# A paced weight cast before the memory keys, a later split of mem, and a last row tile that is normalized in PSUM

## The chip, the cores and the metric

The kernel runs on one core of a Trainium2 chip. The core has engines that each run their own instructions in order: TensorE (matmuls, PE in the profile, with its weight loads as PEld), VectorE (DVE), ScalarE (ACT), GpSimd (POOL), and SyncE (SP), which here issues the DMAs. They wait for each other through semaphores. SBUF is the working memory; PSUM holds what TensorE writes, in banks of 512 fp32 columns. The metric is the device time of one execution in microseconds (us), the median of several runs.

## The reference, cut to what matters

One decoder layer on 256 tokens of width 1024, all in fp32: one input projection feeds a causal pooling mixer and an attention of 8 heads; then come an output projection with LayerNorm, a cross-attention into 256 memory tokens with LayerNorm, and a SwiGLU block with LayerNorm.

```python
z = h @ w_in[l]                                  # u, q, k, v: 512 columns each
pool_out = multiscale_pool(u, w_pool[l], pool_scale[l])
attn_out = moba_attention(q, k, v).reshape(B_, S_, ATTN_WIDTH)
mix = jnp.concatenate([pool_out, attn_out], axis=-1) @ w_out[l]
h = layer_norm(DEEPNORM_ALPHA * h + mix, ln1_g[l], ln1_b[l])
h = layer_norm(DEEPNORM_ALPHA * h + memory_cross_attention(h, mem, w_xq[l], w_xkv[l], w_xo[l]),
               ln2_g[l], ln2_b[l])
h = layer_norm(DEEPNORM_ALPHA * h + swiglu(h, w_gate[l], w_up[l], w_down[l]), ln3_g[l], ln3_b[l])
```

With 256 tokens there is one attention block, so the attention is plain causal attention. The LayerNorm takes the mean and variance of a row of 1024, then `(x - mu) * rsqrt(var + eps) * g + b`.

## The kernel before, in words

**Numbers in two halves.** Every product of weights is made of three matmuls on fp32r halves: a tensor is split into `hi`, its rounded copy, and `lo`, what the copy lost, and hi*hi, hi*lo and lo*hi are added (`three`, line 232; `proj_t`, line 244). The split costs one copy on ScalarE and one subtraction on VectorE (`split`, line 297, and for weights lines 91 and 92).

**The weight stream.** `Stream` (line 42) holds all weights as 125 numbered tiles of [128, 1024] (the first few are half as wide) in the order of use: w0 to w10 for q and k, w11 to w14 for v, w15 to w18 for u, w19 to w26 for the memory keys (`xk`), w27 to w34 for the output projection, and so on. `fetch` issues a load, `prepare` casts a tile into its halves (w12h, w12l in the profile) and then issues the load seven tiles further. There are eight pairs of hi and lo buffers, so a cast waits until the tile eight before it has been used up. `get` is called once for every group of matmuls on a tile: it makes sure that the tile it needs is cast, and, unless the stream is held, asks for one more, up to eight (`AHEAD`) beyond the tiles that are used up. `held` is set in the projections with LayerNorm and in the last part of q and k. `before` hangs further loads onto a tile's load: the load of x for the residual on w27's.

**Order.** Each engine's order is the program's order (`manual_schedule`). The phase that the change touches is written out by hand in lines 500 to 536. `run(gen, n)` advances one of the generators `v`, `u` and `xk` by n steps of matmuls, and between them stand attention's parts:

- a step of `v` is one `get` and three matmuls of 512 columns, for one row tile and one k; there are 16 of them. A step of `u` or `xk` is three matmuls of 256 columns, and every second step calls `get`: 16 calls for u, 32 for the memory keys.
- `scores(hq, t)` (line 402): eight small matmuls into two banks, then on VectorE a masked maximum (line 416), on ScalarE the exponentials (line 385), on VectorE the scaling (lines 390 to 392).
- `probs_t(hp)` (line 426): six transposes into two banks, then a copy of the first bank on VectorE (line 436) and of the second on ScalarE (line 437).
- `attend(hp)` (line 442): four pairs of small matmuls into a bank, then a split.
- `split_mem(k)` (line 188): the split of half of mem's transpose, [128, 1024], a ScalarE copy and a VectorE subtraction; the memory keys read its halves mTh and mTl, the first half in k = 0 to 3, the second in k = 4 to 7.
- `do_v` ends with two copies of v to SBUF on ScalarE (`vt`, line 482); `do_u` copies each of its chunks to `upad` on ScalarE (line 488), from which GpSimd forms the window sums (`windows`, line 455). `pool_diff(g)` (line 465) takes them on VectorE, and `mix_pool(g)` (line 469) multiplies the result on TensorE.

All these parts take banks from one pool of four (`bank`), the projections take theirs from another four (`accbank`).

**The end.** The last projection (`project`, line 589) first adds the first 16 of its 22 weight tiles into four accumulators, one per row tile of 128 tokens and half of the columns; then it finishes piece after piece over the last six tiles. The last row tile's second half is finished as two pieces of 256 columns, and the last of these goes into a bank of its own, so that its sum is that bank plus what the accumulator holds. `Norm` (line 543) adds each piece to the residual on VectorE (line 557), takes statistics (`bn_stats`, line 560), aggregates them (line 565), and forms the reciprocal root on GpSimd (line 568) while VectorE runs the first two `centre`s (line 572); `scale` (line 577) then writes the output row, which is stored in three parts from SyncE's and ScalarE's queues (line 773).

Of the kernel before, what the change touches and what calls it, by code (L numbers as in the profile page):

```python
# [11 lines left out]
OP = mybir.AluOpType  # L12
# [3 lines left out]
D = 1024  # L16
S = 256
T = S // P
# [9 lines left out]
ALPHA = 2.0 ** 0.25  # L28
# [13 lines left out]
class Stream:  # L42


    def __init__(self, nc, pool):
        self.nc, self.pool = nc, pool
        self.src, self.raws, self.tiles, self.homes = [], [], [], []
        self.loads, self.splits = {}, {}
        self.used, self.held = 0, True

    def add(self, src, parts=2):

        n = src.shape[1] // parts
        first = len(self.src)
        self.src += [src[:, i * n:(i + 1) * n, :] for i in range(parts)]
        return range(first, len(self.src))
# [39 lines left out]
    def get(self, numbers, k):  # L96

        n = self.src[numbers[0]].shape[1]
        self.prepare(numbers[k // n] + 1)
        if not self.held:  # L100
            self.prepare(min(self.used + AHEAD, len(self.tiles) + 1))
        hi, lo = self.tiles[numbers[k // n]]
        return hi[:, k % n, :], lo[:, k % n, :]
# [13 lines left out]
def decoder_layer(  # L117
# [3 lines left out]
    nc = tc.nc  # L121
# [13 lines left out]
    def bank(name):  # L135
        return pb.tile([P, 512], F32, tag="b", name=name)

    def accbank(name):
        return pa.tile([P, 512], F32, tag="acc", name=name)


    ws = Stream(nc, wp)
# [45 lines left out]
    def split_mem(k):  # L188
        split(mT[0][:, k:k + 4, :], mT[1][:, k:k + 4, :], mr[0][:, k:k + 4, :])
# [8 lines left out]
    gb = {}  # L198
# [45 lines left out]
    def proj_t(pss, numbers, yT):  # L244


        for k in range(KD):
            hi, lo = ws.get(numbers, k)
            y_hi, y_lo = pair(yT, ALL, k)
            for f in range(2):  # L250
                s = slice(f * P, (f + 1) * P)
                for n, (w, y) in enumerate(((hi, y_hi), (hi, y_lo), (lo, y_hi))):
                    nc.tensor.matmul(pss[f], w[:, s], y, start=k == 0 and f == 0 and n == 0,  # L253
                                     stop=k == KD - 1 and n == 2, skip_group_check=True)
                if f == 1:
                    ws.done(numbers, k)
                yield
# [10 lines left out]
    def proj_rows(acc, chunks, get, pieces, first, last, free, again=False):  # L268

        last_k = sum(ws.rows(numbers) for numbers in chunks) - 1  # L270
        k0 = 0
        for numbers in chunks:
            nk = ws.rows(numbers)
            for t in sorted({piece[0] for piece in pieces}):
                for j in range(nk):
                    k = k0 + j
                    y = pair(get(k), ALL, slice(t * P, (t + 1) * P))
                    hi, lo = ws.get(numbers, j)
                    for piece in pieces:
                        if piece[0] == t:  # L280
                            s = slice(*piece[1:])
                            three(acc[piece], y, (hi[:, s], lo[:, s]), first and k == 0, last and k == last_k,
                                  again)
                    if free and t == pieces[-1][0]:
                        ws.done(numbers, j)
                    yield
            k0 += nk

    def run(gen, n=None):

        while n is None or n > 0:
            if next(gen, gen) is gen:
                return False
            n = None if n is None else n - 1
        return True

    def split(h, l, ps):
        nc.scalar.copy(h, ps)  # L298
        nc.vector.tensor_sub(l, ps, r32(h))  # L299
# [142 lines left out]
    def attend(hp):  # L442
        s0, s1 = pts[hp]
        po = bank("po")
        for j in range(2):
            hs = slice(j * HD, (j + 1) * HD)
            vs = slice((2 * hp + j) * HD, (2 * hp + j + 1) * HD)
            nc.tensor.matmul(po[hs, :S], vt[:, 0, vs], s0[:, j, :], start=True, stop=False)
            nc.tensor.matmul(po[hs, P:S], vt[:, 1, vs], s1[:, j, :], start=False, stop=True)
        split(cT[0][:, 4 + hp, :], cT[1][:, 4 + hp, :], po[:, :S])  # L450
# [14 lines left out]
    def pool_diff(g):  # L465
        pl = upad[:, g, PADW:]
        nc.vector.scalar_tensor_tensor(pl, sums[g][:, PADW:], 1.0 / WINDOWS[g], pl, op0=OP.mult, op1=OP.subtract)
# [9 lines left out]
    def do_v():  # L477
        pieces = [(t, 0, 512) for t in range(T)]
        acc = {piece: accbank("pv") for piece in pieces}
        yield from proj_rows(acc, c_v, lambda k: (xT[0][:, k], xT[1][:, k]), pieces, True, True, True)  # L480
        for piece in pieces:
            nc.scalar.copy(vt[:, piece[0], :], acc[piece])

    def do_u():
        for c in range(2):
            ps = accbank("pu").rearrange("p (f t) -> p f t", f=2)
            yield from proj_t([ps[:, f, :] for f in range(2)], c_u[c], xT)
            nc.scalar.copy(upad[:, 2 * c:2 * c + 2, PADW:], ps)  # L488
            for f in range(2):
                windows(2 * c + f)  # L490
# [3 lines left out]
    def do_xk():  # L494
        for c in range(4):
            ps = accbank("pxk").rearrange("p (f t) -> p f t", f=2)
            yield from proj_t([ps[:, f, :] for f in range(2)], c_xk[c], mT)
            split(xkT[0][:, 2 * c:2 * c + 2, :], xkT[1][:, 2 * c:2 * c + 2, :], ps)

    v, u, xk = do_v(), do_u(), do_xk()  # L500
    run(v, 2)
    scores(0, 0)
    run(v, 2)
    scores(0, 1)
    run(v)
    run(u, 4)
    split_mem(0)
    probs_t(0)
    run(u, 6)
    scores(1, 0)  # L510
    probs_t(1)
    run(u, 6)
    split_mem(4)
    attend(0)
    run(u, 6)
    scores(1, 1)
    attend(1)
    run(u)
    run(xk, 6)
    pool_diff(0)  # L520
# [9 lines left out]
    attend(2)  # L530
    mix_pool(2)
    pool_diff(3)
    run(xk, 8)
    attend(3)
    mix_pool(3)
    run(xk)


    early.close()
# [3 lines left out]
    class Norm:  # L543
# [23 lines left out]
            nc.vector.tensor_scalar(self.rs, self.mv[:, 1:2], EPS, None, op0=OP.add)  # L567
            nc.gpsimd.tensor_tensor(self.rs, self.rs, mhalf, op=OP.pow)  # L568

        def centre(self, c0, c1):  # L570
            s = slice(c0, c1)
            nc.vector.scalar_tensor_tensor(self.r[:, s], self.r[:, s], self.mv[:, 0:1], gb["g", self.i][:, s],  # L572
                                           op0=OP.subtract, op1=OP.mult)

        def scale(self, c0, c1):
            s = slice(c0, c1)
            nc.vector.scalar_tensor_tensor(self.dst[:, s], self.r[:, s], self.rs, gb["b", self.i][:, s],  # L577
                                           op0=OP.mult, op1=OP.add)

        def finish(self):  # L580
            self.stats()
            for half in HALVES:
                self.centre(*half)
                self.scale(*half)

    HALVES = ((0, 512), (512, D))
# [22 lines left out]
    def until(gen):  # L609

        for got in gen:
            if got is not None:
                return got
# [6 lines left out]
    for t in range(T):  # L620
        norm = Norm(1, xt[:, t, :], h1[:, t, :])
# [78 lines left out]
    h2 = ap.tile([P, T, D], F32, tag="a8", name="h2")  # L700
# [14 lines left out]
    norm = Norm(2, h1[:, 0, :], h2[:, 0, :])  # L715
# [3 lines left out]
    norm = Norm(2, h1[:, 1, :], h2[:, 1, :])  # L719
# [52 lines left out]
    def store(t, y, c0, c1, queue=nc.sync):  # L772
        queue.dma_start(out[t * P:(t + 1) * P, c0:c1], y[:, c0:c1])

    pieces = PIECES[:3] + ((1, 512, 768), (1, 768, D))
    dn = project(c_dn, lambda k: (gT[k // KD][0][:, k % KD], gT[k // KD][1][:, k % KD]), 6, pieces)
    run(dn, 4)
    gated_t(NFC - 1)
    for t in range(T):
        norm = Norm(3, h2[:, t, :])  # L780
        for _, c0, c1 in [piece for piece in pieces if piece[0] == t]:
            acc = until(dn)[1]
            if c1 - c0 == 512:
                norm.add(c0, c0 + 256, acc[:, :256])
                norm.add(c0 + 256, c1, acc[:, 256:])
            elif c0 == 512:
                norm.sum(512, D, acc)
                norm.measure(c0, c1)
            else:
                nc.vector.tensor_add(norm.r[:, c0:c1], norm.r[:, c0:c1], acc)  # L790
                norm.measure(c0, c1)
        norm.stats()
        norm.centre(0, 512)
        norm.centre(512, 768)
        norm.scale(0, 512)
        store(t, norm.r, 0, 512)
        norm.scale(512, 768)
        store(t, norm.r, 512, 768, nc.scalar)
        norm.centre(768, D)
        norm.scale(768, D)  # L800
        store(t, norm.r, 768, D)
    run(dn)


# [36 lines left out]
```

## Time and profile before

| | |
|---|---|
| time, median of 3 runs | 389.57 us (389.51 to 389.97) |
| the profiled execution's own time | 389.37 us |
| its span, from the first to the last instruction | 387.6 us |
| TensorE busy | 376.8 us, 97% of the span |
| VectorE, ScalarE, GpSimd busy | 250.5, 179.6, 17.9 us |
| granted TensorE clock, mean | 0.993 |
| read from HBM | 70.52 MB, 185 GB/s over the span |

The profile is one execution, seen by the hardware profiler. A row of the timeline has the start, the duration, the engine, the line of the program, the operation, output and input by the program's names with their shapes, and in brackets the idle time of the engine ahead of it with what ended it. A duration includes the instruction's latency: the next instruction of the same engine often starts before it is over. Rows of waits have the engine and line that waited, what for, the total in us, how often, and the longest. The view by line has the count, the busy time in us and the mean duration in ns. TensorE's matmuls are pipelined, so their busy time is more than their arithmetic.

### The profile page before, as it was taken

The numbers are of one execution on the slowest core, as the hardware profiler recorded it, in microseconds if no ns is written. First come the engines' busy times: TensorE is split into PE (matmuls) and PEld (weight loads), VectorE is DVE, ScalarE is ACT, GpSimd is POOL, SyncE is SP. The second block draws the span as 40 slices with busy tenths as digits, with TensorE's granted clock in tenths as the row PEclk, the third lists the DMA queues.
The fourth block names the chain that finished last, engine by engine and source line by source line (L and its number), as shares of the span: only waits on it lengthen the run. The fifth ranks groups of instructions, "written<-read, shape, count | busy, mean of one in ns | idle before, by whom it ended". The sixth has DMA issues, their size and how long they took to land.

```text
span 387.6 us, 5472 instructions
## 1 busy us (share of the span) xinstructions
PE 376.8 (97%) x2120; PEld 327.4 (84%) x2120; DVE 250.5 (65%) x361; ACT 179.6 (46%) x262; POOL 17.9 (5%) x31
## 2 busy tenths in 40 slices
PE   8999899999999999999999999999999999999992
PEld 8997779998888899988878888888888888888881
DVE  4768998655589767665889655556465555444176
ACT  5656965543254644545148544545554454343000
POOL 1000036100020000000100000000000000000000
PEclk9999999999999999999999999999999999999997
DMA  7998785438507973443108956565557655630011
GB/s 218 400 406 324 221 323 164 145 113 286 200 1 224 402 230 122 128 145 108 56 0 285 364 169 210 167 193 187 183 197 261 225 165 170 212 108 2 0 41 67
DMA packets 21689, 71.91 MB, mean 186 GB/s; under 512 B 2464, under 2 KB 3232, under 8 KB 21536
## 3 DMA queue, kind: packets, MB, share of 16 engines
q1 hardware_dynamic: 21232, 71.05, 53.8%
q10 hardware_dynamic: 432, 0.52, 0.4%
q8 instruction: 16, 0.26, 0.3%
q14 instruction: 9, 0.07, 0.1%
HBM read 70.52 MB, written 1.05 MB: 185 GB/s over the span
## 4 chain that ended last, share of the span: by engine, by line
PE 94%; DVE 4%; issue 1%; POOL 0%; POOLq 0%; ACT 0%; DVEq 0%
PE pg L236 10%; PE pg L235 10%; PE pg L237 10%; PE acc L237 8%; PE acc L236 8%; PE acc L235 8%; PE pqk L349 6%; PE pxq L253 6%; PE pxk L253 6%; PE pu L253 3%; PE xv L237 2%; PE xv L235 2%; PE xv L236 2%; PE pgt L744 1%; PE busy L323 1%; PE pv L235 1%
## 5 line engine op out<-in xcount | busy, mean ns | idle before, releaser
L568 POOL TENSOR_TENSOR rs<-rs,mhalf 128x1 f32<-128x1 f32 x6 | 5.7, 955 | 307.5 <-DVE rs L567 307.5
L737 ACT ACTIVATE sg<-pg 128x256 f32<-128x256 f32 x22 | 8.4, 384 | 12.9 <-PE pg L237 12.8
L557 DVE SCALAR_TENSOR_TENSOR r<-h,acc 128x256 f32<-128x256 f32 (+1 forms) x11 | 5.9, 534 | 10.9 <-PE acc L237 10.9
L738 DVE TENSOR_TENSOR sg<-sg,pg 128x256 f32<-128x256 f32 x22 | 9.3, 421 | 4.0 <-ACT sg L737 2.6
L385 ACT ACTIVATE pr<-pr,mx 128x128 f32<-128x128 f32 (+1 forms) x16 | 7.1, 444 | 7.3 <-DVE mx L416 7.3
L560 DVE BATCH_NORM_STATS2 st<-r 128x6 f32<-128x512 f32 (+1 forms) x16 | 9.0, 561 | 0.5
L572 DVE SCALAR_TENSOR_TENSOR r<-r,mv,g 128x512 f32<-128x512 f32 (+1 forms) x14 | 9.2, 668 | 0.0
L298 ACT CAST h2Th<-tp 128x512 fp32r<-128x512 f32 x4 | 2.4, 588 | 13.7 <-PE tp L309 13.7
L298 ACT CAST gTh<-pgt 128x512 fp32r<-128x512 f32 x11 | 6.0, 589 | 5.8 <-PE pgt L744 5.8
L385 ACT ACTIVATE xpr<-xs,mx 128x256 f32<-128x256 f32 x8 | 3.7, 470 | 10.2 <-DVE mx L396 10.2
L299 DVE TENSOR_TENSOR gTl<-pgt,gTh 128x512 fp32r<-128x512 f32 x11 | 7.1, 687 | 2.0 <-ACT gTh L298 1.5
L577 DVE SCALAR_TENSOR_TENSOR h<-r,rs,b 128x512 f32<-128x512 f32 x8 | 6.0, 752 | 1.9 <-POOL rs L568 1.8
L460 POOL TENSOR_TENSOR win<-upad 128x271 f32<-128x271 f32 x4 | 3.8, 956 | 55.6 <-ACT upad L488 55.6
L744 PEld LDWEIGHTS pgt<-ident,sg 128*128 128x128 f32 x44 | 5.2, 140 | 0.8
L390 DVE RECIPROCAL sm<-sm 128x2 f32<-128x2 f32 x12 | 2.0, 166 | 5.9 <-ACT xpr L385 4.5
L744 PE MATMUL pgt<-ident,sg 128*128 128x128 f32 x44 | 5.8, 272 | 0.0
L309 PEld LDWEIGHTS tp<-ident,h 128*128 128x128 f32 x32 | 3.8, 141 | 2.0 <-issue 0.7
L298 ACT CAST h1Th<-tp 128x512 fp32r<-128x512 f32 x4 | 2.3, 587 | 6.7 <-PE tp L309 6.7
L299 DVE TENSOR_TENSOR xkTl<-pxk,xkTh 128x512 fp32r<-128x512 f32 x4 | 2.8, 692 | 4.1 <-ACT xkTh L298 4.1
L309 PE MATMUL tp<-ident,h 128*128 128x128 f32 x32 | 4.8, 274 | 0.4 <-DVE h L577 0.3
L323 PE MATMUL busy<-spark 128*128 128x128 f32 x18 | 4.2, 430 | 1.1 <-DVE spark L321 1.1
L298 ACT CAST xkTh<-pxk 128x512 fp32r<-128x512 f32 x4 | 2.3, 587 | 5.9 <-PE pxk L253 5.9
(1087 smaller groups left out, 1421.0 us busy)
## 6 DMA issues: line engine op xcount, KB each, us to landing
g<-in_ln_g SPq DMA_DIRECT2D x3, 512.0 KB, 6.4
b<-in_ln_b SPq DMA_DIRECT2D x3, 512.0 KB, 7.4
wr<-in_w_in SPq DMA_DIRECT2D x5, 256.0 KB, 5.8
mr<-in_mem_t SPq DMA_DIRECT2D x1, 1024.0 KB, 11.1
xt<-in_x SPq DMA_DIRECT2D x1, 1024.0 KB, 8.0
xr<-in_x_t SPq DMA_DIRECT2D x3, 256.0 KB, 7.4
wr<-in_w_in SPq DMA_DIRECT2D x1, 512.0 KB, 7.8
w7r<-in_w_in SPq DMA_DIRECT2D x1, 512.0 KB, 8.2
```

Source lines behind the costliest of these rows:

```text
L235: nc.tensor.matmul(ps, wa, ya, start=start, stop=False, skip_group_check=part)
L236: nc.tensor.matmul(ps, wa, yb, start=False, stop=False, skip_group_check=part)
L237: nc.tensor.matmul(ps, wb, ya, start=False, stop=stop, skip_group_check=part)
L253: nc.tensor.matmul(pss[f], w[:, s], y, start=k == 0 and f == 0 and n == 0, stop=k == KD - 1 and n == 2, skip_group_check=True)
L298: nc.scalar.copy(h, ps)
L299: nc.vector.tensor_sub(l, ps, r32(h))
L349: nc.tensor.matmul(qk[i][:, f, :], w[:, c * P:(c + 1) * P], y, start=k == 0 and f == 0 and n == 0 and w is hi, stop=k == KD - 1 and w is l ...
L385: nc.scalar.activation(dst[:, j, :], src[:, j, :], AF.Exp, bias=mx[:, j:j + 1], scale=sign, accum_out=sm[:, j:j + 1])
L560: nc.vector.bn_stats(self.st[:, self.n, :], self.r[:, c0:c1])
L572: nc.vector.scalar_tensor_tensor(self.r[:, s], self.r[:, s], self.mv[:, 0:1], gb["g", self.i][:, s], op0=OP.subtract, op1=OP.mult)
L738: nc.vector.tensor_mul(sg, sg, ps[:, CW:])
L744: nc.tensor.transpose(pt[:, f, t * P:(t + 1) * P], sgs[c][:, t, f * P:(f + 1) * P], ident)
```

## The change

Three things change.

- `Stream` gets a `pace`: a call of `get` asks for a further cast only where the number of calls so far is a multiple of it. It is 3 from v to the memory keys, 2 for the last part of the keys, and 1 otherwise.
- In the hand-written order, `scores(0, 1)` comes after four further steps of v in place of two, and the two `split_mem` come after `attend(0)` and `attend(1)`.
- In the last row tile, the sum with the residual, the statistics and the centring stay in the PSUM banks of the accumulators, in place; only `scale` writes SBUF. The sum of the last 512 columns becomes two of 256.

```diff
@@ class Stream
+        self.pace, self.asked = 1, 0
...
         self.prepare(numbers[k // n] + 1)
-        if not self.held:
+        self.asked += 1
+        if not self.held and self.asked % self.pace == 0:
             self.prepare(min(self.used + AHEAD, len(self.tiles) + 1))
@@ the order from v to the memory keys
     v, u, xk = do_v(), do_u(), do_xk()
+    ws.pace = 3
     run(v, 2)
     scores(0, 0)
-    run(v, 2)
+    run(v, 4)
     scores(0, 1)
     run(v)
     run(u, 4)
-    split_mem(0)
     probs_t(0)
     run(u, 6)
     scores(1, 0)
     probs_t(1)
     run(u, 6)
-    split_mem(4)
     attend(0)
+    split_mem(0)
     run(u, 6)
     scores(1, 1)
     attend(1)
+    split_mem(4)
     run(u)
...
     pool_diff(3)
+    ws.pace = 2
     run(xk, 8)
     attend(3)
     mix_pool(3)
     run(xk)
+    ws.pace = 1
@@ class Norm: centre and scale take the place of the residual
-        def centre(self, c0, c1):
+        def centre(self, c0, c1, r=None):
             s = slice(c0, c1)
-            nc.vector.scalar_tensor_tensor(self.r[:, s], self.r[:, s], self.mv[:, 0:1], gb["g", self.i][:, s],
+            r = self.r[:, s] if r is None else r
+            nc.vector.scalar_tensor_tensor(r, r, self.mv[:, 0:1], gb["g", self.i][:, s],
                                            op0=OP.subtract, op1=OP.mult)
...
+            r = self.r[:, s] if r is None else r
+            nc.vector.scalar_tensor_tensor(self.dst[:, s], r, self.rs, gb["b", self.i][:, s],
                                            op0=OP.mult, op1=OP.add)
@@ the last projection (the first row tile's work stays as it was)
+    def in_bank(norm, acc, c0, c1):
+
+        nc.vector.scalar_tensor_tensor(acc, norm.tok[:, c0:c1], ALPHA, acc, op0=OP.mult, op1=OP.add)
+        nc.vector.bn_stats(norm.st[:, norm.n, :], acc)
+        norm.n += 1
+
+    norm = Norm(3, h2[:, 1, :])
+    left = until(dn)[1]
+    for c in (0, 256):
+        in_bank(norm, left[:, c:c + 256], c, c + 256)
+    right = until(dn)[1]
+    norm.sum(768, D, right[:, 256:])
+    in_bank(norm, right[:, :256], 512, 768)
+    last = until(dn)[1]
+    nc.vector.tensor_add(last, norm.r[:, 768:], last)
+    nc.vector.bn_stats(norm.st[:, norm.n, :], last)
+    norm.n += 1
+    finish(norm, 1, (left, right[:, :256], last))
```

`finish` is what stood behind the sums before, in the same order: statistics, two centres, a scale and its store, a scale and its store, then the last centre, scale and store; its last argument says where the residual's three parts lie.

More of the change, by code (lines that the diff above doesn't have):

```diff
@@ L568, in stats, with scale @@
             nc.gpsimd.tensor_tensor(self.rs, self.rs, mhalf, op=OP.pow)
-        def centre(self, c0, c1):
+        def centre(self, c0, c1, r=None):
             s = slice(c0, c1)
-            nc.vector.scalar_tensor_tensor(self.r[:, s], self.r[:, s], self.mv[:, 0:1], gb["g", self.i][:, s],
+            r = self.r[:, s] if r is None else r
+            nc.vector.scalar_tensor_tensor(r, r, self.mv[:, 0:1], gb["g", self.i][:, s],
                                            op0=OP.subtract, op1=OP.mult)
-        def scale(self, c0, c1):
+        def scale(self, c0, c1, r=None):
             s = slice(c0, c1)
-            nc.vector.scalar_tensor_tensor(self.dst[:, s], self.r[:, s], self.rs, gb["b", self.i][:, s],
+            r = self.r[:, s] if r is None else r
+            nc.vector.scalar_tensor_tensor(self.dst[:, s], r, self.rs, gb["b", self.i][:, s],
                                            op0=OP.mult, op1=OP.add)
@@ L778, in decoder_layer, with finish @@
     gated_t(NFC - 1)
[L779 to L791, printed above, removed]
+    def finish(norm, t, at):
         norm.stats()
-        norm.centre(0, 512)
-        norm.centre(512, 768)
-        norm.scale(0, 512)
+        norm.centre(0, 512, at[0])
+        norm.centre(512, 768, at[1])
+        norm.scale(0, 512, at[0])
         store(t, norm.r, 0, 512)
-        norm.scale(512, 768)
+        norm.scale(512, 768, at[1])
         store(t, norm.r, 512, 768, nc.scalar)
-        norm.centre(768, D)
-        norm.scale(768, D)
+        norm.centre(768, D, at[2])
+        norm.scale(768, D, at[2])
         store(t, norm.r, 768, D)
+    norm = Norm(3, h2[:, 0, :])
+    for half in HALVES:
+        acc = until(dn)[1]
+        for c in (0, 256):
+            norm.add(half[0] + c, half[0] + c + 256, acc[:, c:c + 256])
+    finish(norm, 0, (None, None, None))
+    def in_bank(norm, acc, c0, c1):
[4 more added lines that the diff above has]
+    left = until(dn)[1]
+    for c in (0, 256):
+        in_bank(norm, left[:, c:c + 256], c, c + 256)
[7 more added lines that the diff above has]
+    finish(norm, 1, (left, right[:, :256], last))
     run(dn)
```

## The prediction

> **What bounds the kernel now.** I read the summary by engine, the busy time by stretch of the span, TensorE's waits, and then the timeline around each wait. First the stretches; the columns are the stretch, its length, TensorE's busy time, and then weight loads, VectorE, ScalarE, GpSimd, granted clock and DMA.
>
> ```profile
> 46.00:50.00 4.00, 2.24 (x21) 1.68 (x20) 3.88 (x5) 2.31 (x4) 0.00 (x0) 1.00 0.97 340
> 50.00:198.00 148.00, 148.00 (x954) 132.83 (x953) 104.92 (x164) 68.60 (x113) 14.53 (x18) 1.00 0.50 169
> 198.00:200.00 2.00, 1.61 (x9) 0.88 (x7) 1.97 (x4) 0.62 (x2) 0.00 (x0) 1.00 0.00 0
> 200.00:380.00 180.00, 179.95 (x834) 150.10 (x834) 101.90 (x119) 78.10 (x96) 0.92 (x1) 1.00 0.51 170
> 380.00:387.60 7.60, 0.00 (x0) 0.00 (x0) 4.35 (x10) 0.00 (x0) 0.92 (x1) 0.64 0.19 69
> ```
>
> The reader is to see that TensorE sets the time: from 50 to 380 us it is without work for only 0.39 + 0.05 us. What can be won without fewer matmuls lies in two places, 4.00 - 2.24 = 1.76 us in the stretch from 46 to 50, and the 7.60 us behind the last matmul, where VectorE alone works. The change touches both. TensorE's waits name what stands in the first:
>
> ```profile
> PE pt L433 <- DVE sb L436: 1.3, 1, 1.3
> PE pt L431 <- ACT sb L437: 0.4, 1, 0.4
> ```
>
> Both are the transposes of probs_t(1), which need the banks of probs_t(0), and these are free only when the copies of line 436 (VectorE) and line 437 (ScalarE) have run. The timeline shows why the copies are late:
>
> ```profile
> 37.92 0.42 DVE L416 CUSTOM_DVE_ANT_0 pr<-ps,tri 128x256 f32<-128x256 f32 x1
> ...
> 41.43 1.23 DVE L92 TENSOR_TENSOR w18l<-w18r,w18h 128x1024 fp32r<-128x1024 f32 x1
> ...
> 44.15 1.06 ACT L482 COPY vt<-pv 128x512 f32<-128x512 f32 x2
> ...
> 46.29 0.71 PE L409 MATMUL ps<-qkT 64*128 64x128 f32 x8
> 47.33 1.22 DVE L299 TENSOR_TENSOR mTl<-mr,mTh 128x1024 fp32r<-128x1024 f32 x1
> 47.42 0.33 PE L431 MATMUL pt<-ident,pr 128*128 128x128 f32 x1 [0.41 <-ACT sb L437]
> 48.46 0.68 DVE L436 COPY sb<-pt 128x512 f32<-128x512 f32 x1
> ```
>
> VectorE's queue behind scores(0,1) holds w18, w19, w20, w21, w22 and mem's first half, and only then the copy, at 48.46. A 1024-wide subtraction holds VectorE for 48.46 - 47.33 = 1.13 us. TensorE asked for the banks at 47.42 - 0.41 = 47.01.
>
> **The change, part by part.** *Casts.* A cast is one copy on ScalarE and one subtraction on VectorE, and it lets one load be issued. None is added or removed: I count the calls of get in the program's order. 16 come before v, so with a pace of 3 v's 16 calls ask at the 18th, 21st, 24th, 27th and 30th for w14 to w18 (before: w14 to w21), and u's 16 calls for w19 to w24 (before: w22 to w25). The pace of 2 and the limit of eight ahead bring the count to w33 at the end of the memory keys, as before, so what follows finds the same state. No call has to make a tile that it needs at once: the keys start with w19 to w24 ready.
>
> *The wait at 47 us.* Two casts now stand ahead of scores(0,1) in place of four, so its first row moves from 37.92 to 37.92 - 2 x 1.13 = 35.7, and its last work, which ended just ahead of w18 at 41.43, to 39.2. TensorE gives scores(0,1) two steps later, which hides in what was won. Then come w16, w17, w18 (to 42.6) and w19, whose ScalarE half stands behind v's copies to vt. They started at 44.15 and can now start when v ends, near 42.0: vt to 43.1, w19's copy, which has as many elements as the two of vt, to 44.1, its subtraction to 45.2, and the copy of line 436 ends at 45.9. TensorE asks at 47.0. mem's first half isn't in front any more. So the wait goes, 1.76 us, with 1.1 us to spare; VectorE would have to lose a whole further cast before any of it came back.
>
> *Mem's split, and what is late next.* Rows for the place where the moved work meets TensorE again:
>
> ```profile
> 55.08 1.14 PE L409 MATMUL ps<-qkT 64*128 64x256 f32 x8
> 56.25 0.42 DVE L416 CUSTOM_DVE_ANT_0 pr<-ps,tri 128x256 f32<-128x256 f32 x1
> ...
> 59.55 0.42 DVE L299 TENSOR_TENSOR cTl<-po,cTh 128x256 fp32r<-128x256 f32 x1
> ...
> 60.65 0.28 PE L253 MATMUL pxk<-mTh,w19h 128*128 128x256 f32 x1
> ...
> 60.85 0.59 ACT L488 COPY upad<-pu 128x512 f32<-128x512 f32 x1 [0.85 <-PE pu L253]
> 62.41 1.53 DVE L92 TENSOR_TENSOR w26l<-w26r,w26h 128x1024 fp32r<-128x1024 f32 x1 [1.16 <-ACT w26h L91]
> 63.87 0.85 DVE L467 SCALAR_TENSOR_TENSOR upad<-win,upad 128x256 f32<-128x256 f32 x1
> 65.62 0.60 PE L471 MATMUL pm<-upad,wpl 128*128 128x256 f32 x2
> ```
>
> All of TensorE's times move 1.76 forward. The keys start at 60.65 - 1.76 = 58.9. Mem's first half comes behind w20, scores(1,0), a copy, w21 and attend(0)'s subtraction, at most 45.9 + 1.13 + 3.30 + 0.68 + 1.13 + 0.42 + 1.13 = 53.7 (3.30 is scores(1,1), with wider rows, below). The second follows attend(1): scores(1,1) can start on VectorE when its products are there, 55.08 + 1.14 - 1.76 = 54.5, about when w22 behind mem's first half is done; 3.30 us from row 56.25 to row 59.55 later comes attend(1)'s subtraction (57.8), its 0.42 to 58.2, mem's 1.13 to 59.3. The keys need it after eight steps. Twelve steps and six transposes lie between 60.65 and 65.62, so eight take about 3 us: needed at 61.9. Hidden, by 2.6 us. But behind it on VectorE stand w23, w24 and w25 (3 x 1.13, to 62.7) and then pool_diff(0), without which mix_pool(0) on TensorE can't start. Before, VectorE stood idle here, 1.16 us ahead of w26, and mix_pool(0) came 65.62 - 63.87 - 0.85 = 0.90 after the end of pool_diff(0). Now mix_pool(0) is due at 65.62 - 1.76 = 63.86. pool_diff(0) ends at 62.7 + 0.42 = 63.1 if it runs undisturbed, and its own line says what that is worth:
>
> ```profile
> L467 DVE SCALAR_TENSOR_TENSOR upad<-win,upad x4: 415/416/846, 63.9 to 75.4; 128x256 f32<-128x256 f32 x4
> ```
>
> The 846 ns and the 1.53 us of w26 (1.23 at w18) fall on GpSimd's window sums of the second u chunk, which run here again. With both, pool_diff(0) ends at 62.7 + 0.30 + 0.85 = 63.9, a new wait of about 0.05 us plus a hand-over; with w23, w24 and mem's half slowed in the same way too, 3 x 0.30 more, about 1.0 us. Undisturbed it is 0. I take **0.15 us**, near the case that the rows show, and keep 0 to 1.0. Loads are issued later by as much as their casts, and x's load with them, with no reader near: the first LayerNorm's sum is past 100 us.
>
> *The last row tile.* The rows behind the last matmul, and the same shapes elsewhere (mean ns behind the comma):
>
> ```profile
> 380.04 0.42 DVE L790 TENSOR_TENSOR r<-r,acc 128x256 f32<-128x256 f32 x1 [0.44 <-PE acc L237]
> ...
> 381.32 1.14 DVE L572 SCALAR_TENSOR_TENSOR r<-r,mv,g 128x512 f32<-128x512 f32 x2
> 381.55 0.92 POOL L568 TENSOR_TENSOR rs<-rs,mhalf 128x1 f32<-128x1 f32 x1 [6.68 <-DVE rs L567]
> 382.51 1.15 DVE L577 SCALAR_TENSOR_TENSOR r<-r,rs,b 128x512 f32<-128x512 f32 x2
> ...
> 384.08 0.48 DVE L577 SCALAR_TENSOR_TENSOR r<-r,rs,b 128x256 f32<-128x256 f32 x1
> ```
>
> ```profile
> L557 DVE SCALAR_TENSOR_TENSOR r<-h,acc 128x256 f32<-128x256 f32 x6 | 2.5, 412 | 9.6 <-PE acc L237 9.6
> L473 DVE SCALAR_TENSOR_TENSOR cTl<-pm,psc,cTh 128x256 fp32r<-128x256 f32 x4 | 1.9, 482 | 0.8 <-ACT cTh L472 0.8
> ...
> L572 DVE SCALAR_TENSOR_TENSOR r<-r,mv,g 128x256 f32<-128x256 f32 x4 | 1.9, 480 | 0.0
> ```
>
> The chain keeps its instructions: one addition, one bn_stats, three centres, three scales, the stores. Only the side on which the residual lies changes. Reading a bank in place of SBUF costs nothing that shows: 482 ns with a PSUM input and a per-row scalar against 480 ns without PSUM. Writing a bank from VectorE occurs nowhere in the trace. The nearest rows are two forms of one instruction that differ in their operands, 412 and 480 ns, so I bound it by 0.07 us for each instruction in either direction. A loss counts for all eight, +0.56. A gain counts for six, -0.42, since the first two centres end at 381.32 + 1.14 = 382.46 and the reciprocal root on GpSimd at 381.55 + 0.92 = 382.47: faster centres would wait for it. I take **0**, as the reads show. Ahead of the last matmul one 256-wide instruction is added (the sum of 512 becomes two); VectorE's 0.44 us of idle time ahead of row 380.04 hides its 0.42. With 0.07 us on each of the six instructions there that touch a bank this cover is gone and up to another 0.4 shows.
>
> [...]
>
> **Sum**, on the profiled execution's own 389.37 us (span 387.60 and 1.77 around it): 389.37 - 1.76 + 0.15 + 0 = 387.76. The median of the runs, 389.57, is 0.20 above that execution, so I predict **387.95 us**.
>
> **Rivals.** *The wait moves to mix_pool(0)* (0.13): VectorE's queue stays disturbed by GpSimd, 1.0 us or more comes back: 389.57 - 1.76 + 1.0 = 388.8, in the worst case nothing is left. For it: 1.53 and 846 ns. Against it: three of four pool_diffs took 416 ns. *The copy is late anyway* (0.05), so that the change doesn't do what it says: 389.5. It needs over 1.1 us more on VectorE ahead of it. *A bank costs VectorE more* (0.10), at the bound: +0.56 and 0.2 of the lost cover, 388.7, still faster. [...] *Slower* (0.05): a write into a bank holds VectorE as long as the disturbed pool_diff, 846 - 416 = 430 ns more, on eight instructions: +3.4, 391.2. It decides from (1.76 - 0.15) / 8 = 0.20 us each, and against it stands that no undisturbed row differs so much.
>
> **How the numbers follow.** The forecast has 0.67. What a measurement can tell here is 0.2%, 0.78 us. Faster than 388.79: the forecast, the costly bank and half of the first rival, 0.67 + 0.10 + 0.06 = 0.83. Within: 0.07 + 0.05 = 0.12. Slower: 0.05. The range reaches from the gain at the tail without a new wait, 389.57 - 1.76 - 0.42 = 387.4, to the first rival with a little of the second bound, 388.9.
>
> **What would show it.** Right: no wait of a transpose for line 436 or 437, TensorE busy throughout 46 to 50; at mix_pool(0) a wait of 0 to 0.3 us or none; the keys start near 58.9; the span from the last matmul to the end within 0.1 of 7.6 us. Wrong: TensorE idle by over 0.5 us before the mix, named as waiting for pool_diff, mem's low half or a cast; centres or scales of the last tile that differ by over 0.07 us from 480 ns at 256 columns.

## The result, and the profile after

The changed kernel takes 388.75 us (median of 8 runs, 388.44 to 388.84), the kernel before beside it 389.96 (8 runs, 389.51 to 391.35). The ratio, that of the means, is 0.9962, with a 95% interval of 0.9948 to 0.9976: 1.5 us faster, between 0.9 and 2.0; the medians differ by 1.21 us. That the two kernels differ is clear; by how much, the runs tell less well than the traces do, because the kernel before spreads: of its 59 executions beside the experiments, 23 show a granted clock of 0.989 or 0.990 and take 390.7 to 392.2 us, and the other 36 show 0.993 to 0.997 and take 389.1 to 390.4.

TensorE's waits after the change:

```profile
PE busy L325 <- DVE spark L323: 1.1, 1, 1.1
PE pm L473 <- DVE upad L469: 0.9, 1, 0.9
PE tp L311 <- DVE h L584: 0.3, 1, 0.3
PE pqk L351 <- ACT w4h L92: 0.2, 1, 0.2
```

Both waits of the transposes are gone, and one stands there that wasn't in the list before: mix_pool(0), line 473, waits 0.9 us for pool_diff(0), line 469. (The first and the third row were there before; the last is a weight that arrives late at the very start, w4, whose copy on ScalarE waited 0.95 us for its load; TensorE waited 0.2 us for it here, 0.8 in run 6, and run 3 lists no such wait.) By stretches, with the columns as before:

```profile
46.00:50.00 4.00, 4.00 (x37) 3.75 (x37) 3.27 (x16) 2.29 (x11) 0.00 (x0) 1.00 0.94 320
58.90:66.00 7.10, 6.21 (x51) 5.92 (x51) 7.04 (x7) 5.08 (x8) 4.15 (x4) 1.00 0.42 130
66.00:196.00 130.00, 130.00 (x813) 116.49 (x812) 91.75 (x125) 58.45 (x87) 7.61 (x9) 1.00 0.50 171
```

From 46 to 50 TensorE now works throughout, where it had stood idle for 1.76 us. The copy of the first bank runs well ahead of the transposes of probs_t(1):

```profile
45.32 0.68 DVE L438 COPY sb<-pt 128x512 f32<-128x512 f32 x1
...
47.40 0.33 PE L433 MATMUL pt<-ident,pr 128*128 128x128 f32 x1
47.56 0.27 PE L434 MATMUL pt<-ident,pr 128*128 128x128 f32 x1
47.67 0.27 PE L435 MATMUL pt<-ident,pr 128*128 128x128 f32 x1
...
48.03 0.36 PE L255 MATMUL pu<-xTh,w16h 128*128 128x256 f32 x1
```

From 58.9 to 66 it misses 0.89 us, while VectorE is busy for 7.04 of 7.10; from 66 to 196 nothing is missing. The timeline of that place, VectorE's rows first, then GpSimd's and TensorE's:

```profile
52.64 1.22 DVE L301 TENSOR_TENSOR mTl<-mr,mTh 128x1024 fp32r<-128x1024 f32 x1 [0.36 <-ACT mTh L300]
54.07 1.37 DVE L93 TENSOR_TENSOR w22l<-w22r,w22h 128x1024 fp32r<-128x1024 f32 x1 [0.21 <-ACT w22h L92]
...
59.20 1.22 DVE L301 TENSOR_TENSOR mTl<-mr,mTh 128x1024 fp32r<-128x1024 f32 x1
60.34 1.22 DVE L93 TENSOR_TENSOR w23l<-w23r,w23h 128x1024 fp32r<-128x1024 f32 x1
61.48 1.22 DVE L93 TENSOR_TENSOR w24l<-w24r,w24h 128x1024 fp32r<-128x1024 f32 x1
62.61 1.66 DVE L93 TENSOR_TENSOR w25l<-w25r,w25h 128x1024 fp32r<-128x1024 f32 x1
64.20 0.85 DVE L469 SCALAR_TENSOR_TENSOR upad<-win,upad 128x256 f32<-128x256 f32 x1
...
61.62 1.58 POOL L462 TENSOR_TENSOR win<-upad 128x271 f32<-128x271 f32 x1 [4.49 <-ACT upad L490]
63.27 2.26 POOL L462 TENSOR_TENSOR win<-win 128x269 f32<-128x269 f32 x2
...
65.10 0.70 PE L473 MATMUL pm<-upad,wpl 128*128 128x256 f32 x2 [0.89 <-DVE upad L469]
```

Mem's second half, three casts and pool_diff(0) stand in one unbroken queue, and the last two are slow (1.66 us where a cast takes 1.22, 0.85 where a pool_diff takes 0.42) while GpSimd's window sums run beside them. The first sum starts beside w24, which keeps its 1.22 us; there it is the sum that is long, 1.58 us against 0.64 for the same sum in run 11. The end of the kernel, VectorE's and GpSimd's rows:

```profile
379.60 0.43 DVE L820 TENSOR_TENSOR acc<-r,acc 128x256 f32<-128x256 f32 x1
...
380.90 1.14 DVE L578 SCALAR_TENSOR_TENSOR acc<-acc,mv,g 128x512 f32<-128x512 f32 x2
381.95 1.14 DVE L584 SCALAR_TENSOR_TENSOR r<-acc,rs,b 128x512 f32<-128x512 f32 x2
...
383.52 0.48 DVE L584 SCALAR_TENSOR_TENSOR r<-acc,rs,b 128x256 f32<-128x256 f32 x1
...
381.13 0.55 POOL L573 TENSOR_TENSOR rs<-rs,mhalf 128x1 f32<-128x1 f32 x1 [6.70 <-DVE rs L572]
```

VectorE's own instructions take what they took (0.43 us for the addition against 0.42, 1.14 for two centres as before, 1.14 for two scales against 1.15); GpSimd's reciprocal root takes 0.55 us where it had taken 0.92. The scales now start 1.05 us after the centres, before it was 382.51 - 381.32 = 1.19.

The start of a profiled execution varies: v's first matmul starts between 28.89 us (before) and 29.69 (runs 6 and 8), and the list of TensorE's waits has none for the first weights in the kernel before and 1.4 us in run 6. So two spans can't be compared closely. Distances inside an execution can. The table has the start of three of TensorE's matmuls, counted from the first matmul of v, and the distance from the last matmul's start to the last scale's. "Keys" is the first matmul of the memory keys. All are differences of timeline rows, each run from its own profile; 1.05 is the delay of mix_pool(0) against the runs in which nothing holds it (34.70).

| run | keys | mix_pool(0) | last matmul | tail |
|---|---|---|---|---|
| before | 31.76 | 36.73 | 350.83 | 4.36 |
| changed | 29.72 | 35.75 | 349.94 | 4.23 |
| front only (1) | 29.72 | 35.75 | 349.96 | 4.36 |
| tail only (2) | 31.77 | 36.74 | 350.82 | 4.24 |
| pool_diff early (3) | 29.72 | 34.70 | 348.84 | 4.23 |
| order, no pace (4) | 31.00 | 35.98 | 350.06 | 4.24 |
| pace, old order (5) | 29.71 | 34.69 | 348.81 | 4.24 |
| window sums later (11) | 29.72 | 34.87 | 349.12 | 4.24 |

The change gives 2.04 us ahead of the keys, loses 1.05 at mix_pool(0) (with small differences, 0.89 remain to the last matmul), and gains 0.13 behind it: 1.02 us from v on, inside the interval of the runs.

### The profile page after: what moved, and what is told of

Its sections match the earlier page's. It is cut to its first block, busy times and chain, and to the rows that moved or that the text cites. A ratio compares the mean times of both kernels' runs of the same rounds, so it can differ in the third digit from the quotient of the medians.

```text
span 387.0 us, 5476 instructions
## 1 busy us (share of the span) xinstructions
PE 377.0 (97%) x2120; PEld 327.5 (85%) x2120; DVE 251.5 (65%) x362; ACT 179.8 (46%) x262; POOL 19.3 (5%) x31
## 3 DMA queue, kind: packets, MB, share of 16 engines
HBM read 70.52 MB, written 1.05 MB: 185 GB/s over the span
## 4 chain that ended last, share of the span: by engine, by line
PE 88%; DVE 5%; DMA 2%; ACT 2%; issue 1%; SPq 1%; POOL 0%; DVEq 0%; POOLq 0%; ACTq 0%
PE pg L239 10%; PE pg L237 10%; PE pg L238 10%; PE acc L237 8%; PE acc L239 8%; PE acc L238 8%; PE pxq L255 6%; PE pxk L255 5%; PE pqk L351 5%; DMA wr<-in_w_in 2%; PE xv L239 2%; PE xv L237 2%; PE xv L238 2%; PE pu L255 1%; PE pgt L751 1%; PE pv L237 1%
## 5 line engine op out<-in xcount | busy, mean ns | idle before, releaser
L562 DVE SCALAR_TENSOR_TENSOR r<-h,acc 128x256 f32<-128x256 f32 (+1 forms) x9 | 4.8, 532 | 10.9 <-PE acc L239 10.9
L578 DVE SCALAR_TENSOR_TENSOR r<-r,mv,g 128x512 f32<-128x512 f32 (+1 forms) x11 | 7.6, 695 | 0.0
L565 DVE BATCH_NORM_STATS2 st<-r 128x6 f32<-128x512 f32 (+1 forms) x12 | 7.3, 605 | 0.4
L462 POOL TENSOR_TENSOR win<-win 128x269 f32<-128x269 f32 (+2 forms) x6 | 6.0, 993 | 0.5
L305 DVE SCALAR_TENSOR_TENSOR xq<-pxq,xq 128x512 fp32r<-128x512 f32 x4 | 2.8, 691 | 3.3 <-ACT xq L304 3.3
```

The source lines that it names most:

```text
L462: nc.gpsimd.tensor_add(nxt[:, 2 * n - 1:], cur[:, 2 * n - 1:], cur[:, n - 1:PADW + S - n])
```

## The experiments

Each is the changed kernel with one edit, except run 2, which is the kernel before with one; they are timed against the kernel before, and the ratio has its 95% interval.

**1, front only.** The last row tile as before the change, everything else changed.

> The pace and the new order, with the last row tile as before. Theory: the front gives 1.2 us (1.8 us of idle time and about 0.2 of restarts gone at the transposes of probs_t(1), 0.9 given back at mix_pool(0)), the tail gives 0.1; so about 1.2 us faster than before, with TensorE waiting 0.7 to 1.0 us for pool_diff(0), and the reciprocal root on GpSimd back at 0.92 us. Rival: the tail gives more than its chain shows; then this run is less than 0.8 us faster than before.

388.80 us, ratio 0.9962 (0.9946 to 0.9979). The wait at mix_pool(0) is 0.9 us again and the root takes 0.92; the tail is back at 4.36 us. So nearly all of what the runs measure is the front's.

**2, tail only.** The kernel before, with the last row tile in its banks.

> The old order and casts, with only the last row tile in its banks. Theory: 0.1 us faster than before, within what can be measured: the addition behind the last matmul to the end of the last scale takes 4.4 us against 4.52, since the reciprocal root takes 0.55 us against 0.92 and the centres are then the later of the two. TensorE still waits 1.76 us near 47 us. Rival: the tail is worth 0.5 us or more.

389.69 us, ratio 0.9986 (0.9968 to 1.0005): not told from no change, and the rival of 0.5 us isn't excluded by the times alone. By the trace the tail is 0.12 us shorter, and TensorE's waits of 1.3 and 0.4 us at the transposes are as before.

**3, pool_diff(0) early.**

```diff
     attend(1)
+    pool_diff(0)
     split_mem(4)
     run(u)
-    run(xk, 6)
-    pool_diff(0)
-    run(xk, 6)
+    run(xk, 12)
```

> The changed kernel with pool_diff(0) ahead of mem's second half on VectorE, so that it stands before the casts w23, w24 and w25. Theory (the wait at mix_pool(0) is VectorE's queue): that wait of 0.9 us goes, 0.8 to 1.0 us faster than the changed kernel, some 2.2 us faster than before. Rival (the window sums on GpSimd or the matmuls' own data are late): the wait stays, same time as the changed kernel. Second rival: mem's second half, now 0.4 to 0.9 us later, holds the memory keys; then a wait appears at them, less than 0.5 us.

387.42 us, ratio 0.9934 (0.9914 to 0.9954), 1.3 us under the changed kernel in the medians. In VectorE's rows of this run pool_diff(0) takes 0.42 us at 58.85, mem's half follows, and mix_pool(0) stands behind the transposes without a gap:

```profile
58.85 0.42 DVE L469 SCALAR_TENSOR_TENSOR upad<-win,upad 128x256 f32<-128x256 f32 x1
59.18 1.22 DVE L301 TENSOR_TENSOR mTl<-mr,mTh 128x1024 fp32r<-128x1024 f32 x1
```

```profile
63.73 0.27 PE L435 MATMUL pt<-ident,pr 128*128 128x128 f32 x1
63.84 0.38 PE L473 MATMUL pm<-upad,wpl 128*128 128x256 f32 x1
```

So the data were long there, and VectorE's queue was what held mix_pool(0). The keys don't wait for mem's half (the second rival).

**4, the new order without the pace.** The three lines that set `ws.pace` left out.

> The changed kernel without the pace: casts are asked at every call, the order stays new. Theory (pace and order both matter): three casts w20 to w22 and four ahead of scores(0,1) leave the copy of line 438 about 0.7 us after the time at which the transposes of probs_t(1) ask; a wait of 0.5 to 1.0 us there. At mix_pool(0) less than 0.5 us, since that wait only moves the same queue against TensorE. In all within 0.5 us of the changed kernel. Rival (the pace does nothing): no wait at the transposes.

388.84 us, ratio 0.9965 (0.9951 to 0.9979), the changed kernel's time. Six casts stood ahead of scores(0,1) on VectorE, where there had been four before the change and are two under the pace, and TensorE waited at the transposes:

```profile
PE pt L435 <- DVE sb L438: 1.1, 1, 1.1
```

1.1 us is a little over what was expected, from a count of four casts ahead of scores(0,1) where there are six. mix_pool(0) doesn't wait, since TensorE comes to it 1.3 us later than in the changed kernel (31.00 against 29.72 at the keys).

**5, the pace with the old order.** scores(0,1) after two steps and both halves of mem where they had been.

> The pace with the old order (scores(0,1) after two steps, mem's halves where they were); the last row tile as changed. Theory (each of pace and order takes work from in front of the copy): mem's first half stands ahead of the copy again, one subtraction of 1.13 us, which eats the 1.1 us to spare; a wait of 0.1 to 0.6 us at the transposes, and the wait at mix_pool(0) stays at 0.4 to 1.0 us, since VectorE has the same work ahead of pool_diff(0). Time within 0.5 us of the changed kernel. Rival (the order does all): the wait at the transposes is 1 us or more.

387.85 us, ratio 0.9941 (0.9923 to 0.9960). Theory and rival were both wrong: there is no wait at the transposes and none at mix_pool(0). This was the surprise of the study, and VectorE's rows show the reason:

```profile
45.38 1.22 DVE L301 TENSOR_TENSOR mTl<-mr,mTh 128x1024 fp32r<-128x1024 f32 x1
46.51 0.68 DVE L438 COPY sb<-pt 128x512 f32<-128x512 f32 x1
...
52.60 1.22 DVE L301 TENSOR_TENSOR mTl<-mr,mTh 128x1024 fp32r<-128x1024 f32 x1
...
59.16 1.23 DVE L93 TENSOR_TENSOR w23l<-w23r,w23h 128x1024 fp32r<-128x1024 f32 x1
...
63.02 0.85 DVE L469 SCALAR_TENSOR_TENSOR upad<-win,upad 128x256 f32<-128x256 f32 x1
```

At 52.6 us VectorE runs mem's second half here and mem's first half in the changed kernel (52.64), and both come to scores(1,1) at the same time (55.33 and 55.36). The old order is one subtraction ahead at that point, so w23 stands at 59.16 where the changed kernel has mem's second half (59.20), and pool_diff(0) starts 1.18 us earlier. The subtraction that the new order moved away from the copy of probs_t(0) had run in time in which VectorE otherwise waits for ScalarE and TensorE; moved, it lands in the one full stretch. (From w19 to scores(1,1) VectorE is idle for 1.30 us in the changed kernel and for 0.48 here.) And the copy is in time even behind mem's first half, at 46.51.

**6, window sums behind pool_diff(0).** A first try to take GpSimd's work from beside VectorE's queue: `run(u, 10)` in place of `run(u)`, and the rest of u, which is the copy to upad and the sums, behind pool_diff(0).

> The changed kernel with the copy of u's second chunk to upad, and so its window sums on GpSimd, behind pool_diff(0). Theory (part of the wait at mix_pool(0) is VectorE slowed by the window sums: 1.66 us for w25 against 1.23, 0.85 for pool_diff(0) against 0.42): w25 takes 1.23 and pool_diff(0) 0.42, the wait falls from 0.89 to 0.0 to 0.2 us, and 0.7 to 0.9 us are won over the changed kernel, unless the later window sums hold mix_pool(2) in their turn. Rival (the queue's length alone): w25 and pool_diff(0) are as slow as before and the wait stays at 0.7 us or more.

388.92 us, ratio 0.9961 (0.9946 to 0.9976), wait 0.91 us. The edit didn't do what it was made for: it moves the copy only behind w25's on ScalarE, the sums started at 62.91, and w25 (1.68 us) and pool_diff(0) (0.85) ran beside them as before. The rival's numbers came, but since the sums weren't out of the way, the run decides nothing.

**7 and 8, one half of the tail each.** In 7 the centres read the banks but write SBUF. In 8 the sums stay in SBUF, the centres read SBUF and write the banks.

```diff
-            nc.vector.scalar_tensor_tensor(r, r, self.mv[:, 0:1], gb["g", self.i][:, s],
+            nc.vector.scalar_tensor_tensor(self.r[:, s], r, self.mv[:, 0:1], gb["g", self.i][:, s],
```

```diff
-            nc.vector.scalar_tensor_tensor(r, r, self.mv[:, 0:1], gb["g", self.i][:, s],
+            nc.vector.scalar_tensor_tensor(r, self.r[:, s], self.mv[:, 0:1], gb["g", self.i][:, s],
...
-        nc.vector.scalar_tensor_tensor(acc, norm.tok[:, c0:c1], ALPHA, acc, op0=OP.mult, op1=OP.add)
+        nc.vector.scalar_tensor_tensor(norm.r[:, c0:c1], norm.tok[:, c0:c1], ALPHA, acc, op0=OP.mult, op1=OP.add)
```

> The changed kernel, but the last tile's centres read the banks and write SBUF, and the scales read SBUF. Theory (GpSimd's reciprocal root is slowed by VectorE reading two SBUF tensors beside it): the centres read only g from SBUF, so the root stays at 0.55 us. Rival (it is slowed by VectorE writing SBUF): 0.92 us.

> The other half: the sums and the statistics in SBUF as before the change, the centres read SBUF and write the banks, the scales read the banks. Theory (two SBUF reads slow the root): 0.92 us, and the chain behind the last matmul takes 4.5 us as before the change. Rival (writes slow it): 0.55 us.

One execution each (388.89 and 389.35 us), too few for a time. First run 7's centres and root, then run 8's:

```profile
380.99 1.13 DVE L578 SCALAR_TENSOR_TENSOR r<-acc,mv,g 128x512 f32<-128x512 f32 x2
...
381.22 0.55 POOL L573 TENSOR_TENSOR rs<-rs,mhalf 128x1 f32<-128x1 f32 x1 [6.69 <-DVE rs L572]
```

```profile
381.31 1.15 DVE L578 SCALAR_TENSOR_TENSOR acc<-r,mv,g 128x512 f32<-128x512 f32 x2
...
381.54 0.92 POOL L573 TENSOR_TENSOR rs<-rs,mhalf 128x1 f32<-128x1 f32 x1 [6.69 <-DVE rs L572]
```

With the changed kernel and the one before these are all four cases: 0.55 with a bank as the source whatever the destination, 0.92 with two SBUF sources whatever the destination. The distance from the last matmul to the last scale goes with it, 4.23 us in run 7 and 4.36 in run 8. So in these four the root's time goes with VectorE's second read of SBUF and not with where VectorE writes, and this is where the tail's 0.13 us come from.

**9 and 10, the order taken apart.** Both with the pace. In 9 scores(0,1) come after four steps and mem's halves stand as before; in 10 scores(0,1) come after two steps and mem's halves are late.

> The pace, scores(0,1) after four steps, mem's halves where they stood before the change; last row tile as changed. Theory (mem's later split makes the wait at mix_pool(0): in the run with the old order its halves ran in time in which VectorE otherwise stands idle): no wait at mix_pool(0), none or under 0.3 us at the transposes; 0.7 to 1.2 us faster than the changed kernel. Rival (the later scores(0,1) make it): 0.9 us at mix_pool(0), the time of the changed kernel.

> The pace and mem's later halves, scores(0,1) after two steps as before the change. Theory: 0.8 to 1.0 us of wait at mix_pool(0) for pool_diff(0), none at the transposes, the time of the changed kernel within 0.3 us. Rival: no wait, 0.7 to 1.2 us faster than the changed kernel.

9: 387.90 us, ratio 0.9927 (0.9903 to 0.9951), no wait at either place. 10: 388.76 us, ratio 0.9956 (0.9939 to 0.9972), 0.9 us at mix_pool(0), by run 10's list of waits:

```profile
PE pm L473 <- DVE upad L469: 0.9, 1, 0.9
```

The later split of mem makes the wait; the place of scores(0,1) does nothing under the pace.

**11, window sums later still.** `run(u, 10)`, and the rest of u behind the transposes of probs_t(2).

> The changed kernel, u's second copy to upad and its window sums behind the transposes of probs_t(2), whose bank's copy stands ahead of them on ScalarE, so that they can't start ahead of about 65 us. Theory (w25 and pool_diff(0) are slowed by GpSimd reading SBUF beside them): they take 1.23 and 0.42 us, pool_diff(0) ends 0.8 us sooner, the wait at mix_pool(0) is 0.0 to 0.2 us, and what is won is 0.7 to 0.9 us unless the sums come too late for mix_pool(2) or (3). Rival (the queue alone): w25 and pool_diff(0) as slow as in the changed kernel, wait 0.9 us.

387.87 us, ratio 0.9935 (0.9913 to 0.9957). This time the sums start behind pool_diff(0); VectorE's rows, then GpSimd's:

```profile
62.85 1.22 DVE L93 TENSOR_TENSOR w25l<-w25r,w25h 128x1024 fp32r<-128x1024 f32 x1
63.99 0.42 DVE L469 SCALAR_TENSOR_TENSOR upad<-win,upad 128x256 f32<-128x256 f32 x1
...
65.48 0.64 POOL L462 TENSOR_TENSOR win<-upad 128x271 f32<-128x271 f32 x1 [8.11 <-ACT upad L490]
```

Both instructions are back at 1.22 and 0.42 us, and mix_pool(0) comes 0.17 us after its undisturbed distance in place of 1.05. So the wait needed two causes together, and taking either away is enough to remove all of it (runs 5 and 9) or most of it (here): the queue was one subtraction too long, and its last two instructions were slowed by 0.4 us each.

**What beats both.** Runs 3, 5 and 9 have no wait left between v and the mix: about 1.1 us between v and the last matmul, by the table, better than the changed kernel (run 9's first keys and mix stand at 29.72 and 34.70). The trace doesn't tell them apart. The simplest is 5, the pace without a new order, with the last row tile in its banks.

## Why the prediction was right or wrong

- **The wait of the transposes: right, and 0.28 us larger.** The copy of the first bank stood at 45.32 in an execution that was 0.46 us late from the start, so 44.9 in the times of the prediction, which had it end at 45.9 and so start near 45.2. The idle time of 1.76 us went, but the keys came 2.04 us sooner. The trace of before shows the rest as busy: from 47.01 to u's next matmul at 49.61 it had been 2.60 us for six transposes, and it is now 48.03 - 47.40 = 0.63. The rows of before:

```profile
49.20 0.33 PE L433 MATMUL pt<-ident,pr 128*128 128x128 f32 x1 [1.35 <-DVE sb L436]
...
49.61 0.36 PE L253 MATMUL pu<-xTh,w16h 128*128 128x256 f32 x1
```

- **Casts: right.** No cast was late for its matmuls, and the phase behind the mix is the same. That the pace alone would do, run 5, was not foreseen; "mem's first half isn't in front any more" was named as part of the cause, and it wasn't needed: in run 5 the copy at 46.51 is in time behind it.
- **Mem's split and what is late next: the place was right, the size was not.** "I take 0.15 us" failed: the wait cost 1.05, and the prediction's own sign of being wrong, over 0.5 us of idle time before the mix that waits for pool_diff, was met (0.89). In the prediction's times pool_diff(0) ended at 65.05 - 0.46 = 64.6, not at 63.9, and mix_pool(0) was due at 28.89 + 34.70 = 63.6, not at 63.86. The later end has two parts. scores(1,1) started at 55.36 - 0.46 = 54.9 on VectorE, not at 54.5, since the working took w22 as "about" done and counted no idle time for mem's first half and w22, which waited 0.36 and 0.21 us for ScalarE. The rest are w25's 1.66 us against the 1.53 that was put in, and hand-overs of the queue between. That GpSimd's sums would slow both instructions was put in rightly (1.66 and 0.85 us beside them, 1.22 and 0.42 in run 11). The first rival, with 1.0 us at this place, is the size that came, and its 388.8 us is the time that was measured; but the way to it was another, since mem's half, w23 and w24, whose slowing made up that 1.0 us, took 1.22 us each as in quiet stretches.
- **The last row tile: no cost, as forecast, but a gain of 0.13 us that came another way.** "Faster centres would wait for" the root: the root itself became faster, 0.55 us against 0.92, and nothing in the row of before said so. By this gain the span behind the last matmul is 7.4 us, a little outside the 7.6 within 0.1 that was named. The bound of 0.07 us for each write to a bank was wide: the addition into a bank took 430 ns against 422 into SBUF, and the sum with the residual 426 against 412. The centres that read and write a bank took 484 ns at 256 columns, those of before 480. Runs 7 and 8 show what the root's time goes with: 0.55 us where the centres beside it read a bank, 0.92 where they read only SBUF.
- **The sum.** 1.62 us were forecast; the runs give 1.5 by the ratio (0.9 to 2.0) and 1.21 by the medians, the trace 1.02 from v on. That the time, 388.75 us against 387.95, stayed within the range is in part luck, since the errors have opposite signs: 0.28 and 0.13 more gained, 0.9 more given back at mix_pool(0) and 0.1 behind it. What the runs show beyond the trace goes with the granted clock of the kernel before. Without its two executions above 391 us, which take as long as those at 0.989 do, its median is 389.76, 1.0 us above the changed kernel's, as in the trace. A clock of 0.989 or 0.990 was seen only where TensorE has the whole wait of 1.76 us near 47 us: in 23 of the 59 executions of the kernel before, in 2 of 12 of run 2, and in none of 74 of the changed kernel and the other timed runs. The change may have won this as well; no trace of such an execution is kept, and why its clock is lower isn't shown.

## What to carry to other kernels

Work that is taken from in front of a late copy has to be put into time in which its engine waits; put behind, it can make the next consumer late. Here the pace with the old order was 1.13 us better, by the table, than the pace with the new one. An engine's queue ahead of a hand-over is to be added up from the trace with its own waits and with what GpSimd runs beside it, since two instructions beside the window sums took 0.4 us more each than in quiet stretches. And keeping one of VectorE's operands in its PSUM bank was worth 0.37 us to the GpSimd instruction beside it, of which 0.13 us reached the end of the kernel.

## What the runs showed of the hardware

A stall of TensorE cost more than the idle time that the profile gives it: 1.76 us idle, 2.04 us of delay, and 0.89 idle at mix_pool(0) for 1.05 of delay. Idle time counts from the end of a matmul, while in an unbroken row of transposes, each of 0.27 us, the next one starts 0.11 us after the start of the one before; these 0.16 us of each stall count as busy, and run 11's delay of 0.17 us shows as no wait at all. VectorE's instructions of 256 columns that write a bank took within 14 ns of the same ones that write SBUF: 426 against 412, 430 against 422, 484 against 480. And the last row tile's reciprocal root, one value per partition on GpSimd, took 0.55 us in the changed kernel and in runs 2 to 7, where VectorE's centres beside it read a bank, and 0.92 in the kernel before and in runs 1 and 8, where they read only SBUF; where the centres wrote made no difference (runs 7 and 8).
